# A state space's convolution input, taken out of the attention filler and given a phase of its own with seven products for four

## The chip, the cores and the metric

The kernel runs on one core of a Trainium2 chip. The metric is the device time of one execution in microseconds (us); lower is better. Before the change three runs took 2005.05, 2005.51 and 2002.23 us, median 2005.05.

The engines go by these names: PE is TensorE (matrix products; PEld its weight loads), DVE is VectorE, ACT is ScalarE, POOL is GpSimd, and SP is the queue that starts most DMAs.

## What is computed

One block of a hybrid encoder on x of 1024 tokens by 1024 features. The normalized input is multiplied by one wide matrix `w_in`; its columns feed latent attention (MLA, 8 heads), forgetting attention (fox, 8 heads), a Mamba-2 state space (SSD) and the gates that merge the three. Then an output projection and a gated FFN with a convolution. What the change touches is the input of the state space, 1536 columns, and the three gates, 3072 columns:

```python
hn = rms_norm(x, norm_mix_g[l])
u = hn @ w_in[l]
u_mla, u_fox, u_ssm, u_gate = jnp.split(u, split_at, axis=-1)
...
z, xBC, dt_raw = jnp.split(u, [SSM_INNER, SSM_INNER + SSM_XBC], axis=-1)
xBC = jax.nn.silu(causal_dwconv(xBC, conv_w, conv_b))
...
g = jax.nn.sigmoid(u_gate + b_gate[l]).reshape(Bsz, S, N_BRANCH, D_MODEL)
```

`causal_dwconv` has four taps along the tokens, a weight of its own for each column and tap.

## The kernel before, in words

Every float32 product is made of three passes on PE: both operands are split into a rounded high part (h, made by ACT) and the rest (l, made by DVE), and h·h, h·l and l·h are summed in PSUM. The normalized input, transposed, stays in SBUF as `hnh` and `hnl`, each in two halves of 512 tokens and 8 slices of 128 features. One block of 128 output columns costs 2 halves x 8 slices x 3 passes = 48 matmuls of 128x128 by 512.

The stages in time: norm and MLA projections to about 200 us; four chunks of 512 columns for fox and z, eight token units each (L798), to 384; attention to about 903; the state space to 1094; the branch outputs (L1729), the output projection (L1865), the FFN up (L1820) and down (L2161). In the chunks, `gate_sums` makes the forget gates' running sums on DVE, `down_sums` makes sums of FFN down weights on POOL at the units that `DOWN_FOX` lists, `out_z` finishes a z unit with a tanh, and `qk_sum`, `qk_pair` and `qk_out` normalize, transpose and split the fox queries and keys. In the FFN up projection, pairs of column blocks are made by seven half-size block products in place of eight (Strassen-Winograd), from sums of weights and of tokens.

**Attention** walks 16 heads, each in four units of two rows of 128 queries. A row of scores (`score_row`, matmuls L1296) has one chunk up to row four and two chunks from row five on, in a ring of three PSUM banks, tag "s". DVE takes the maximum of a chunk (L1301 for the first, L1312 for the last), the smaller of two negated ones (L1314), ACT the exponential (L1319), which frees the bank, DVE the sum's reciprocal (L1324, L1325), POOL the normalization (L1326). Later PE transposes (L1384), ACT and DVE split (L1389, L1390), and PE multiplies by the values (L1349 to L1357).

**The filler.** Between these matmuls stand others that depend on nothing in attention: `all_fill` makes 36 blocks, 12 of convolution input and 24 of gates, 48 matmuls each (L1179), as a generator. `merge` interleaves the streams of a unit by their share of work done; the filler's share is a number times the cost of the unit's own work, `FILL_ATT` in attention and `FILL_SSD` in the state space. The PE order is therefore written by the program; the orders of DVE, ACT, POOL and SP are chosen by a scheduler. A filled block is finished off PE: a gate by a tanh on ACT (L1158) and a store, a convolution block by `conv_done`: a copy (L1184), the bias and the first tap on POOL (L1144), three taps in two halves each on DVE (L1137), a tanh on ACT (L1150), a product on DVE (L1141). The weights of every block are split at L1122 (ACT) and L1123 (DVE).

Of the kernel before, what the change touches and what calls it, by code (L numbers as in the profile page):

```python
# [16 lines left out]
ALU = mybir.AluOpType  # L17
# [25 lines left out]
def block_kernel(ctx: ExitStack, tc: tile.TileContext, x, positions, norm_mix_g, w_in, b_gate,  # L43
# [83 lines left out]
    def uid(s):  # L127
        cnt[0] += 1
        return f"{s}_{cnt[0]}"
# [801 lines left out]
    def down_sums(tiles):  # L931
# [11 lines left out]
        for c, s_ in ((0, s12), (2, s34)):  # L943
            down_stores.append(lambda c=c, s_=s_: tc.keep_in_program_order(
                SY.dma_start(wsum_d[k, :, c:c + 2, :], s_)))

    with ExitStack() as px:
        xp = px.enter_context(TP("xp", 2))
# [21 lines left out]
        def getter(w, n, i):  # L970
            if n % 2:
                return lambda k: w[i][:, k, :]
            return lambda k: w[0][i][:, k, :] if k < 4 else w[k // 2 - 1][i][:, k % 2, :]

        def out_z(p, t, zc):
            th = xp.tile([P, 512], F32, name=uid("th"), tag="fsq")
            A.activation(th, p, AF.Tanh, scale=0.5)
            zt = xp.tile([P, 512], F32, name=uid("zt"), tag="fqn", bufs=4)
            V.scalar_tensor_tensor(out=zt, in0=th, scalar=1.0, in1=p, op0=ALU.add, op1=ALU.mult)
            SY.dma_start(z_d[t * P:(t + 1) * P, zc:zc + 512], zt)  # L980

        def qk_sum(p, ss):
            sq = xp.tile([P, 512], F32, name=uid("fsq"), tag="fsq")
            A.activation(sq, p, AF.Square)
            V.reduce_sum(ss, sq.rearrange("p (h d) -> p h d", d=64), axis=AX)
# [31 lines left out]
        for n, (which, c0) in enumerate(chunks):  # L1017
            wh, wl = getter(w, n, 0), getter(w, n, 1)
            w = []
            for t in range(NT):  # L1020
# [24 lines left out]
                if units >= 8:  # L1045
                    next(sums, None)
    pf.close()
    pjp.close()
    order0.__exit__(None, None, None)


# [17 lines left out]


    psg = ctx.enter_context(ExitStack())
    psf = psg.enter_context(TP("psfill", 2, space=PSUM))
# [3 lines left out]
    def later(us, fn):  # L1076
        h = [clk[0] + us, uid(""), fn]
        queue.append(h)
        return h
# [45 lines left out]

    def conv_done(j, u, ul, t0):
        a, al = f_t4.get()
        t = [t0]

        def step(us, fn):  # L1130
            h = later(t[0], fn)
            t[0] += us
            return h

        def tap(d, c0, c1):
            w = pc_g[:, 24 + 12 * (3 - d) + j:25 + 12 * (3 - d) + j]
            return lambda: pin(V.scalar_tensor_tensor(out=a[:, c0:c1], in0=u[:, c0 - d:c1 - d], scalar=w,  # L1137
                                                      in1=a[:, c0:c1], op0=ALU.mult, op1=ALU.add))

        def out(c0, c1):  # L1140
            return lambda: pin(V.scalar_tensor_tensor(out=u[:, c0:c1], in0=u[:, c0:c1], scalar=1.0, in1=a[:, c0:c1],  # L1141
                                                      op0=ALU.add, op1=ALU.mult))

        step(1.4, lambda: G.tensor_scalar(a, u, pc_g[:, 60 + j:61 + j], pc_g[:, 72 + j:73 + j],  # L1144
                                          op0=ALU.mult, op1=ALU.add))
        for d in (1, 2, 3):
            for c0, c1 in ((512, S), (d, 512)):
                step(2.0, tap(d, c0, c1))
        for c0, c1 in ((0, 512), (512, S)):
            step(1.6, lambda c0=c0, c1=c1: pin(A.activation(u[:, c0:c1], a[:, c0:c1], AF.Tanh)))  # L1150
        step(1.1, out(0, 512))
        al[0] = step(1.0, out(512, S))
        ul[0] = step(0.0, lambda: SY.dma_start(xbc_d[j], u))

    gate_behind = [None]
# [6 lines left out]
    def all_fill():  # L1162

        conv = [("c", j, C_XBC + j * P) for j in range(12)]
        gates = [(b, j, C_G + b * D + j * P) for b in (1, 0, 2) for j in range(NK)]
        blocks = [e for n in range(12) for e in (conv[n], gates[n])] + gates[12:]
        nxt = fill_load(blocks[0][2], True)
        for n, (kind, j, c0) in enumerate(blocks):
# [5 lines left out]
            for half in range(2):  # L1174
                ps, pl = f_ps.get()
                hs = slice(512 * half, 512 * half + 512)
                for k in range(NK):
# [3 lines left out]
                    if (k + 1) % grain[0] == 0 and k < NK - 1:  # L1181
                        yield 0.65 * grain[0]
                if kind == "c":
                    fn = lambda ps=ps, hs=hs, u=u: A.activation(u[:, hs], ps, AF.Copy)  # L1184
                else:
                    fn = lambda ps=ps, hs=hs, u=u, r=8 * kind + j: gate_tanh(u[:, hs], ps, pc_g[:, r:r + 1])
                wait = 50.0 if n == len(blocks) - 1 and half == 1 else 0.0
                pl[0] = later(wait + 1.4, fn)
                if half == 1:
                    if kind == "c":  # L1190
                        conv_done(j, u, ul, 2.2)
                    else:
                        ul[0] = later(wait + 2.0, lambda u=u, g=g_d[kind][j]: SY.dma_start(g, u))
                yield 0.65 * grain[0]
# [226 lines left out]

    FILL_ATT = 1.08
    FILL_SSD = [11.3] * 8 + [12.0, 24.5]
# [790 lines left out]
```

## Time and profile before

| what | us |
|---|---|
| median of three runs | 2005.05 |
| span of the profiled execution (a run of 2005.05 has some 3 us around it) | 2002.0 |
| PE busy | 1977.5 |
| DVE, ACT, POOL busy | 1365.9, 944.5, 651.9 |
| filler matmuls L1179, share of the chain that ended last | 19% |
| chunks of fox and z | about 198 to 384.5 |
| attention | 384.5 to about 903 |
| state space | about 904 to 1094 |

How to read the profile: one execution is recorded. A row of the timeline has start, length, engine, line, operation, what is written <- what is read, and in brackets the idle time ahead of it and what ended that. A row of the windows has the stretch, then busy time and number of instructions of PE, PEld, DVE, ACT and POOL, then the granted PE clock, the DMA share and GB/s. A row of groups has line, engine, operation, number | busy time, mean ns of one | idle time ahead and its releasers. A piece of the chain has start, length and what ran. Matmuls are pipelined: one of 512 columns shows as 390 ns and the next starts 227 ns after it.

### The profile page before, as it was taken

The numbers are of one execution on the slowest core, as the hardware profiler recorded it, in microseconds if no ns is written. First come the engines' busy times: TensorE is split into PE (matmuls) and PEld (weight loads), VectorE is DVE, ScalarE is ACT, GpSimd is POOL, SyncE is SP. The second block draws the span as 40 slices with busy tenths as digits, with TensorE's granted clock in tenths as the row PEclk, the third lists the DMA queues.
The fourth block names the chain that finished last, engine by engine and source line by source line (L and its number), as shares of the span: only waits on it lengthen the run. The fifth ranks groups of instructions, "written<-read, shape, count | busy, mean of one in ns | idle before, by whom it ended". The sixth has DMA issues, their size and how long they took to land.

```text
span 2002.0 us, 28702 instructions
## 1 busy us (share of the span) xinstructions
PE 1977.5 (99%) x10185; PEld 1676.7 (84%) x10185; DVE 1365.9 (68%) x2345; ACT 944.5 (47%) x1778; POOL 651.9 (33%) x636
## 2 busy tenths in 40 slices
PE   8999999999999999999999999999999999999998
PEld 7989888888888888888888888888888888888887
DVE  7777567267666677656885476568997777666665
ACT  5555323255555556557775132225454444544432
POOL 5133322021212223213331252100764544423764
PEclk9999999999999999999999999999999999999999
DMA  5166857543535444427654786433332211249575
GB/s 178 52 195 210 277 179 224 165 125 105 139 114 145 122 120 133 125 78 238 183 192 139 259 284 202 144 119 107 104 95 90 78 55 53 78 159 337 188 262 185
DMA packets 278265, 312.18 MB, mean 156 GB/s; under 512 B 19197, under 2 KB 209289, under 8 KB 278122
## 3 DMA queue, kind: packets, MB, share of 16 engines
q1 hardware_dynamic: 278120, 310.35, 49.6%
q8 instruction: 80, 1.31, 0.3%
q14 instruction: 63, 0.52, 0.1%
q10 hardware_dynamic: 2, 0.00, 0.0%
HBM read 217.17 MB, written 93.13 MB: 155 GB/s over the span
## 4 chain that ended last, share of the span: by engine, by line
PE 86%; DVE 4%; issue 3%; DMA 3%; POOL 2%; ACT 2%; SPq 1%; ACTq 0%; DVEq 0%; POOLq 0%
PE mm L1179 19%; PE fx L798 9%; PE dn L2161 8%; PE ybr L1729 7%; PE ua L1820 6%; PE uc L1820 5%; PE ud L1820 4%; PE wo L1865 4%; PE s L1296 4%; PE tp L1384 3%; PE ub L1820 2%; PE fxv L188 2%; PE py L1574 1%; PE o L1357 1%; PE ckv L517 1%
## 5 line engine op out<-in xcount | busy, mean ns | idle before, releaser
L1326 POOL TENSOR_SCALAR pm<-pm,rs 128x128 f32<-128x128 f32 (+7 forms) x128 | 105.3, 826 | 413.9 <-DVE rs L1325 290.1
L1179 PE MATMUL mm<-hnh,wh 128*128 128x512 f32 x576 | 236.9, 411 | 0.0
L1179 PE MATMUL mm<-hnh,wl 128*128 128x512 f32 x576 | 226.0, 392 | 0.0
L1179 PE MATMUL mm<-hnl,wh 128*128 128x512 f32 x576 | 225.8, 392 | 0.0
L2161 PE MATMUL dn<-dr,dr 128*128 128x512 f32 x592 | 182.3, 389 | 0.0
L1319 ACT ACTIVATE pm<-s,nmx 128x128 f32<-128x128 f32 (+2 forms) x192 | 110.4, 581 | 64.9 <-DVE nmx L1314 61.4
L2161 PEld LDWEIGHTS dn<-dr,dr 128*128 128x128 f32 x592 | 111.1, 188 | 23.0
L1179 PEld LDWEIGHTS mm<-hnh,wl 128*128 128x128 f32 x576 | 108.1, 188 | 24.6
L1179 PEld LDWEIGHTS mm<-hnl,wh 128*128 128x128 f32 x576 | 108.9, 189 | 15.6
L1179 PEld LDWEIGHTS mm<-hnh,wh 128*128 128x128 f32 x576 | 108.8, 189 | 15.5
L1390 DVE TENSOR_TENSOR ptl<-tp,pth 128x512 fp32r<-128x512 f32 (+1 forms) x160 | 98.4, 633 | 32.8 <-ACT pth L1389 30.7
L1389 ACT ACTIVATE pth<-tp 128x512 fp32r<-128x512 f32 (+1 forms) x160 | 84.8, 555 | 72.6 <-PE tp L1384 72.5
L2161 PE MATMUL dn<-dr 128*128 128x512 f32 x296 | 115.3, 389 | 1.1 <-DVE dY L2178 1.1
L135 DVE TENSOR_TENSOR dr<-dr,dr 128x1024 fp32r<-128x1024 f32 x52 | 75.8, 1465 | 49.1 <-ACT dr L134 47.2
L1729 PE MATMUL ybr<-ah,wl 128*128 128x512 f32 x256 | 99.7, 390 | 1.1 <-DVE wl L135 1.1
L1729 PE MATMUL ybr<-al,wh 128*128 128x512 f32 x256 | 99.8, 390 | 0.0
L1729 PE MATMUL ybr<-ah,wh 128*128 128x512 f32 x256 | 99.7, 389 | 0.0
L134 ACT ACTIVATE dr<-dr 128x1024 fp32r<-128x1024 f32 x52 | 55.1, 1061 | 73.0 <-PE dn L2161 50.0
L1312 DVE TENSOR_REDUCE nmx<-s 128x1 f32<-128x384 f32 (+3 forms) x128 | 65.8, 518 | 32.7 <-PE s L1296 19.1
L134 ACT ACTIVATE wh<-wr 128x1024 fp32r<-128x1024 f32 (+1 forms) x40 | 35.1, 877 | 98.1 <-PE ybr L1729 45.9
L1384 PE MATMUL tp<-ident,pm 128*128 128x128 f32 x576 | 79.8, 273 | 0.6 <-POOL pm L1326 0.6
L135 DVE TENSOR_TENSOR wl<-S,wh 128x1024 fp32r<-128x1024 f32 x42 | 63.2, 1504 | 23.3 <-ACT wh L134 23.3
(531 smaller groups left out, 5782.7 us busy)
## 6 DMA issues: line engine op xcount, KB each, us to landing
dr<-act_d SPq DMA_DIRECT2D x99, 256.0 KB
wr<-in_w_in_dram SPq DMA_DIRECT2D x36, 512.0 KB
g_d<-t SPq DMA_DIRECT2D x24, 512.0 KB
gl<-g_d SPq DMA_DIRECT2D x24, 512.0 KB
wr<-in_ffn_w_up_dram SPq DMA_DIRECT2D x23, 512.0 KB
ws<-in_ffn_w_down_dram SPq DMA_DIRECT2D x22, 512.0 KB
wsum_d<-ws SPq DMA_DIRECT2D x22, 512.0 KB
act_d<-fa SPq DMA_DIRECT2D x22, 512.0 KB
```

Source lines behind the costliest of these rows:

```text
L134: i = A.activation(h, src, AF.Copy) if he is A else he.tensor_copy(h, src)
L135: return i, le.tensor_sub(l, src, f32(h))
L798: T.matmul(p, a(k), b(k), start=k == 0 and i == 0, stop=k == NK - 1 and i == 2)
L1179: T.matmul(ps, a[:, k, :], b[half][:, k, :], start=(k == 0 and i == 0), stop=(k == NK - 1 and i == 2))
L1319: pss[cj][1][0] = later(t0 + 0.9 + 0.1 * cj, lambda cj=cj, a_=a_, b_=b_: A.activation(p_[:, a_:b_], pss[cj][0][:, :b_ - a_], AF.Exp, bias= ...
L1326: G.tensor_scalar(p_[:, 0:n * P], p_[:, 0:n * P], rs[:, 3:4], 0.0, op0=ALU.mult, op1=ALU.add)
L1384: T.transpose(pt[:, off:off + P], pn[qi][0][:, k * P:k * P + P], ident)
L1389: later(cs + 0.05, lambda th=th, pt=pt, off=off: A.activation(th[:, :off], pt[:, :off], AF.Copy))
L1390: pl[0] = later(cs + 0.6, lambda th=th, tl=tl, pt=pt, off=off: V.tensor_sub(tl[:, :off], pt[:, :off], f32(th[:, :off])))
L1729: T.matmul(pss[half], w_[:, k, :], a_[k][:, hs], start=k == 0 and i == 0, stop=k == nk - 1 and i == 2)
L1820: T.matmul(ps, a, b, start=first and n == 0, stop=n == 11, skip_group_check=not first)
L2161: T.matmul(ps[m], a[:, ts_], b[:, 512:], start=first_ and j == 0 and q == 0, stop=j == NFH - 1 and q == 2, skip_group_check=not first_)
```

## The change

The 12 convolution blocks leave the filler. They are made in a phase between the last chunk and attention, in six pairs: blocks n and n + 6, by seven products of 12 matmuls each with half the depth and half the tokens (504 matmuls, L1186 of the changed kernel, in place of 576). The token sums T1 to T4 that this needs are made by `token_sums` during the third and fourth chunk (DVE, two operations on POOL, ACT splits), the weights and sums of the first pair by `conv_first` in the fourth; so the gate sums are drained before the third chunk, and `DOWN_FOX` moves to earlier units. The convolution's taps run on full rows of 1024 on DVE, with bias and first tap on ACT and Silu in place of tanh and product. The filler is left with 24 gate blocks; `FILL_ATT` goes from 1.08 to 0.50, `FILL_SSD` stays. 588 of the filler's matmuls stand in attention (1206 before) and 564 behind it (522 before).

```diff
+    def token_sums():
...
+        u = {k: stage() for k in (0, 2)}
+        for k in (0, 2):
+            G.tensor_sub(u[k], b(hnl, 1, k + 4), b(hnl, 1, k))
+        yield
+        for k in (0, 2):
+            V.tensor_add(u[k], u[k], b(hnh, 1, k + 4))
+            V.tensor_sub(u[k], u[k], b(hnh, 1, k))
+            yield
+            fine(T3_, k, u[k])
+            yield
+        for k in (0, 2):
+            V.tensor_add(u[k], u[k], b(hnh, 0, k))
+            V.tensor_add(u[k], u[k], b(hnl, 0, k))
+            T4f.append(stage())
+            fine(T2_, k, u[k])
+            yield
+            V.tensor_sub(T4f[-1], b(hnh, 0, k + 4), u[k])
+            V.tensor_add(T4f[-1], T4f[-1], b(hnl, 0, k + 4))
+            V.tensor_sub(u[k], b(hnh, 1, k + 4), u[k])
+            V.tensor_add(u[k], u[k], b(hnl, 1, k + 4))
+            fine(T1_, k, u[k])
+            yield
...
-        DOWN_FOX = (2, 6, 10, 14, 18, 21)
+        DOWN_FOX = (1, 4, 7, 10, 13, 16)
...
+                if n == 2 and t >= 2 or n == 3:
+                    next(token3, None)
+                if n == 3:
+                    next(first_c, None)
...
+        def conv(j, c):
+            a = fpl.tile([P, S], F32, name=uid("ca"), tag="t4", bufs=4)
+            A.activation(a, c, AF.Identity, bias=pc_g[:, 72 + j:73 + j], scale=pc_g[:, 60 + j:61 + j])
+            for d in (1, 2, 3):
+                w = pc_g[:, 24 + 12 * (3 - d) + j:25 + 12 * (3 - d) + j]
+                V.scalar_tensor_tensor(out=a[:, d:], in0=c[:, :S - d], scalar=w, in1=a[:, d:],
+                                       op0=ALU.mult, op1=ALU.add)
+            A.activation(a, a, AF.Silu, scale=2.0)
+            SY.dma_start(xbc_d[j], a)
...
+        for n in range(6):
...
+            a0, b0, c0_, d0 = (c_bank() for _ in range(4))
+            c_product(a0, hA, 0, B11)
+            e1 = cg[:, 512:]
+            A.activation(e1, a0, AF.Copy)
+            steps_ = [lambda: c_product(b0, hS12, 4, T2c), lambda: c_product(a0, hA, 4, B21, False),
+                      lambda: c_product(c0_, hS12, 0, T1c)]
+            for i in (1, 2, 0) if n == 0 else (0, 1, 2):
+                steps_[i]()
...
-        conv = [("c", j, C_XBC + j * P) for j in range(12)]
-        gates = [(b, j, C_G + b * D + j * P) for b in (1, 0, 2) for j in range(NK)]
-        blocks = [e for n in range(12) for e in (conv[n], gates[n])] + gates[12:]
+        blocks = [(b, j, C_G + b * D + j * P) for b in (1, 0, 2) for j in range(NK)]
...
-    FILL_ATT = 1.08
+    FILL_ATT = 0.50
```

Three places in the orders. The first is on PE, inside attention's fifth head: rows five and six of its scores. Before, with `s_6413` the second chunk of row five, `s_6420` and `s_6440` the two chunks of row six:

```order
L1296 MATMUL s_6413<-w0h_5800,w0l_5801 128x256 x3
L1296 MATMUL s_6420<-w0h_5800,w0l_5801 128x384 x3
L1349 MATMUL o<-pth_6354,vv_5696 128x256
L1351 MATMUL o<-pth_6354,vv_5696 128x256
L1352 MATMUL o<-ptl_6355,vv_5696 128x256
L1357 MATMUL o<-ptl_6355,vv_5696 128x256
L1179 MATMUL mm_6364<-hnh_119,wh_5982 128x512
L1179 MATMUL mm_6364<-hnl_121,wh_5982 128x512
L1179 MATMUL mm_6364<-hnh_119,wl_5983 128x512
...
L1296 MATMUL s_6440<-w0h_5800,w0l_5801 128x384 x3
```

The same place now, with `s_7091`, `s_7099` and `s_7111` in these roles:

```order
L1441 MATMUL s_7091<-w0h_6561,w0l_6562 128x256 x3
L1441 MATMUL s_7099<-w0h_6561,w0l_6562 128x384 x3
L1494 MATMUL o<-pth_7039,vv_6477 128x256
L1496 MATMUL o<-pth_7039,vv_6477 128x256
L1497 MATMUL o<-ptl_7040,vv_6477 128x256
L1502 MATMUL o<-ptl_7040,vv_6477 128x256
L1441 MATMUL s_7111<-w0h_6561,w0l_6562 128x384 x3
```

The six filler matmuls between the two chunks of row six are gone; the four value matmuls (o) are still there.

The second place is on DVE, in the fourth chunk, ahead of the last normalized keys (`fqn`; `fr` and `rs_t` belong to their root, `fsl` are the split keys of the pair before). Before:

```order
L166 TENSOR_TENSOR rs_t_4352<-fr_843_4338 128x16
L167 TENSOR_TENSOR rs_t_4352<-rs_t_4352,rs_v_4342 128x16
L168 SCALAR_TENSOR_TENSOR fr_843_4338<-rs_t_4352,fr_843_4338 128x16
L994 TENSOR_TENSOR fqn_4356<-fx_4239,fr_843_4338 128x512
L994 TENSOR_TENSOR fqn_4358<-fx_4295,fr_843_4338 128x512
```

Now, with the token sums `Tf` and the low part `T2l` among them:

```order
L140 TENSOR_TENSOR T2l<-Tf_4190,T2h 128x1024
L1074 SCALAR_TENSOR_TENSOR fsl_4459<-tp_4453,fk_col,fsh_4458 128x512
L972 TENSOR_TENSOR Tf_4611<-Tf_4611,hnl_120 128x1024
L168 SCALAR_TENSOR_TENSOR fr_845_4356<-rs_t_4366,fr_845_4356 128x16
L157 TENSOR_SCALAR rs_i_4472<-fv_865_4469 128x16
L160 TENSOR_SCALAR rs_v_4475<-fv_865_4469 128x16
L973 TENSOR_TENSOR Tf_4190<-hnh_119,Tf_4190 128x1024
L166 TENSOR_TENSOR rs_t_4370<-fr_845_4356 128x16
L158 TENSOR_SCALAR fr_866_4471<-rs_i_4472 128x16
L974 TENSOR_TENSOR Tf_4190<-Tf_4190,hnl_121 128x1024
...
L1062 TENSOR_TENSOR fqn_4374<-fx_4267,fr_845_4356 128x512
```

Operations of 1024 elements now stand between the small ones of the root that the keys need.

The third place is on DVE where attention begins. Before, after the last z units (`zt`):

```order
L979 SCALAR_TENSOR_TENSOR zt_4732<-th_4730,fx_4705 128x512
L979 SCALAR_TENSOR_TENSOR zt_4762<-th_4760,fx_4735 128x512
L1312 TENSOR_REDUCE nmx_4836<-s_4838 128x1
L1312 TENSOR_REDUCE nmx_4844<-s_4846 128x1
L1325 RECIPROCAL rs_4837<-rs_4837 128x1
```

Now, with `cg_5563` and `cv_5659` the last pair's two blocks and `ca` their convolutions:

```order
L1247 TENSOR_TENSOR cg_5563<-cb_5566,X_5645 128x512
L1197 SCALAR_TENSOR_TENSOR ca_5665<-cg_5563,pc_g,ca_5665 128x1023
L1248 TENSOR_TENSOR cv_5659<-cb_5567,X_5645 128x512
L1197 SCALAR_TENSOR_TENSOR ca_5665<-cg_5563,pc_g,ca_5665 128x1022
L1197 SCALAR_TENSOR_TENSOR ca_5665<-cg_5563,pc_g,ca_5665 128x1021
L1197 SCALAR_TENSOR_TENSOR ca_5672<-cv_5659,pc_g,ca_5672 128x1023
L1197 SCALAR_TENSOR_TENSOR ca_5672<-cv_5659,pc_g,ca_5672 128x1022
L1197 SCALAR_TENSOR_TENSOR ca_5672<-cv_5659,pc_g,ca_5672 128x1021
L1457 TENSOR_REDUCE nmx_5750<-s_5752 128x1
```

Eight operations of the last pair now stand between the product phase and the first maximum.

More of the change, by code (lines that the diff above doesn't have):

```diff
@@ L1124, in fill_load @@
         return h, l, rl
[L1126 to L1153, printed above, removed]
     gate_behind = [None]
@@ L1189, in all_fill @@
                 if half == 1:
[L1190 to L1193, printed above, removed]
+                    ul[0] = later(wait + 2.0, lambda u=u, g=g_d[kind][j]: SY.dma_start(g, u))
                 yield 0.65 * grain[0]
```

136 lines of the change are left out of this document (127 added, 9 removed).

## The prediction

> **What bounds the kernel now.** I read the page first: engine totals, then the chain of work that ended last.
>
> ```profile
> span 2002.0 us, 28702 instructions
> PE 1977.5 (99%) x10185; PEld 1676.7 (84%) x10185; DVE 1365.9 (68%) x2345; ACT 944.5 (47%) x1778; POOL 651.9 (33%) x636
> PE 86%; DVE 4%; issue 3%; DMA 3%; POOL 2%; ACT 2%; SPq 1%; ACTq 0%; DVEq 0%; POOLq 0%
> ```
>
> TensorE is busy for 99% of the span, and the chain runs over it for 86%. So a matmul taken away is time taken away, as long as what is left still covers the waits that those matmuls cover today. The windows over the first part of attention show the same, with the other engines at about two thirds and a half, and the clock column at 1.00:
>
> ```profile
> 390.00:513.00 123.00, 121.52 (x709) 106.19 (x708) 81.32 (x195) 69.38 (x174) 29.30 (x37) 1.00 0.48 129
> ```
>
> The chain gives the price of one matmul of 512 columns: pieces of the filler in attention, and a long unbroken stretch.
>
> ```profile
> 384.68 5.44 PE mm L1179 x24
> 571.99 2.76 PE mm L1179 x12
> 1150.66 119.52 PE ybr L1729 x526
> ```
>
> 119.52/526 = 0.227 us in a long stretch, 2.76/12 = 0.230 us for twelve between other work. I work against the profiled execution, span 2002.0; the median of the runs is 2005.05, so 3.05 lies around the span, and I add it at the end.
>
> **Term A, the count.** The filler loses 12 blocks of 48 matmuls, 576. At 0.230 that is 132.5 us. The new phase issues 6 pairs x 7 products x 12 = 504 at 0.227, 114.4. Difference −18.1; there are also some 50 fewer places in attention where PE turns from transposes to filler, and I allow 0.03–0.05 us for each. **A = −20** (bounds −16.4, which is 72 x 0.227, and −22). The 42 filler matmuls that merely move from attention to the state space are in neither count.
>
> **Term B, chunk 3.** The token sums put 22 VectorE operations of 128x1024 beside the last two projection chunks, 21 of them between about 306 us and the last normalized keys. What VectorE does there today:
>
> ```profile
> 316.00:340.00 24.00, 24.00 (x115) 19.80 (x114) 19.79 (x42) 8.87 (x13) 8.39 (x7) 1.00 0.71 220
> 340.00:350.00 10.00, 10.00 (x50) 8.34 (x49) 8.83 (x21) 2.10 (x4) 3.64 (x2) 1.00 1.03 280
> 350.00:360.00 10.00, 10.00 (x49) 8.27 (x48) 2.67 (x4) 3.04 (x5) 0.00 (x0) 1.00 0.93 290
> ```
>
> ```profile
> L140 DVE TENSOR_TENSOR w5l<-raw,w5h 128x1024 fp32r<-128x1024 f32 x4 | 4.9, 1215 | 0.0
> L985 DVE TENSOR_REDUCE fss<-fsq 128x8 f32<-128x512 f32 x7 | 4.8, 682 | 6.9 <-ACT fsq L984 6.9
> ```
>
> VectorE (third pair) is busy for 19.79 of 24 and 8.83 of 10 already. In the order of after, 86 rows stand from the first token sum to fqn_4376: 21 of 128x1024 at about 1.15–1.2 (25 us), 7 reduces at 0.6, 7 fsl and 6 fqn at 0.6–0.7, some 45 small ones at 0.1–0.2: about 44 us without a gap. They can start at about 306, when GpSimd's two subtractions are there (they stand behind a load of down weights; today the same load leads to the GpSimd group at 315.97). So the last normalized keys are there at about 350–351. Today they are ready at 332:
>
> ```profile
> 331.43 1.29 DVE L994 TENSOR_TENSOR fqn<-fx,fr 128x512 f32<-128x512 f32 x2
> ```
>
> In the PE order their transposes stand right behind unit 24 of the 32, which ends at 339.20 + 5.50 = 344.7 (the next unit's piece is the second row):
>
> ```profile
> 339.20 5.50 PE fx L798 x24
> 345.58 5.47 PE fx L798 x24
> ```
>
> PE would have to wait from 344.7 to about 350.7; the 12 us of slack that cover this today are spent. **B = +6.** The lower bound is 3: the small operations, 45 of them, are taken 0.07 us shorter each. For the upper bound, what VectorE loses beside GpSimd:
>
> ```profile
> 317.23 1.30 POOL L940 TENSOR_TENSOR ws<-ws,ws 128x512 f32<-128x512 f32 x1
> ```
>
> ```profile
> 317.34 1.22 DVE L157 TENSOR_SCALAR rs_i<-fv 128x16 int32<-128x16 int32 x1
> 328.50 0.17 DVE L157 TENSOR_SCALAR rs_i<-fv 128x16 int32<-128x16 int32 x1
> ```
>
> The same small operation takes 1.22 us while a GpSimd subtraction runs and 0.17 without. Two loads of down weights, with four subtractions each, fall into the stretch; if three of the eight meet a small operation, 3 us more: 9. The Trainium skill, SBUF — State Buffer, "Who interferes with whom", has a rule for this: VectorE and GpSimd share a pair of ports under an exclusive lock, and the loser waits for the other's whole instruction. By that rule, the trace agrees in these three rows.
>
> **Term C, start of the phase.** In pair 0 the second product goes into the bank of the first (a0, first with B11 and then with B21), and must wait until ScalarE has copied the first out. That copy stands behind the last tanh and four splits, three of 1024 elements and one of 512:
>
> ```profile
> 384.72 0.60 ACT L977 ACTIVATE th<-fx 128x512 f32<-128x512 f32 x1 [4.84 <-PE fx L798]
> ```
>
> ```profile
> L134 ACT ACTIVATE wh<-S 128x1024 fp32r<-128x1024 f32 x20 | 21.2, 1062 | 31.3 <-PE uc L1820 31.3
> ```
>
> From the phase's start the copy ends after 0.6 + 1.06 + 0.6 + 2 x 1.06 + 0.6 = 5.0 us, the first product after 12 x 0.227 = 2.7. **C = +2.4** (1, if one split runs before the last tanh, to 4.5, if the two of T4 also wait for their VectorE half). The next product, waiting behind it on PE, needs T2 and a split that are long done.
>
> **Inside the phase** I charge nothing. Its nearest relative is the up projection of the FFN, which makes the same seven products per pair, with other sums:
>
> ```profile
> 1520.00:1600.00 80.00, 80.00 (x355) 66.24 (x354) 61.36 (x52) 38.96 (x46) 39.73 (x26) 1.00 0.25 80
> ```
>
> ```profile
> L2038 DVE SCALAR_TENSOR_TENSOR fa<-cg,pc_f,fa 128x1022 f32<-128x1022 f32 x11 | 24.4, 2216 | 0.0
> L2038 DVE SCALAR_TENSOR_TENSOR fa<-cv,pc_f,fa 128x1023 f32<-128x1023 f32 x11 | 14.0, 1273 | 0.0
> L2046 ACT ACTIVATE fa<-fa 128x1024 f32<-128x1024 f32 x11 | 11.7, 1061 | 16.1 <-DVE fa L2038 16.1
> ```
>
> 84 x 0.227 = 19.07 us a pair for PE. In those 80 us (4.2 pairs) VectorE is busy 14.6 us a pair, GpSimd 9.5, ScalarE 9.3, and PE never pauses. The convolution adds two taps (1.27 to 2.22 us each) and drops one product of 1.28: 15.9 to 17.8 a pair, under 19.07.
>
> **Term D, start of attention.** The last pair's tail (two sums, six taps) stands on VectorE ahead of attention's first maximum; on ScalarE two Silu and a table load stand ahead of the first exponential.
>
> ```profile
> L2046 ACT ACT_TABLE_LOAD x1 | 1.3, 1283 | 0.0
> ```
>
> Two sums of 0.7 (the reduce of 512 above takes 0.68) and six taps of 1.27–1.4 make 9.3 to 9.8 us behind the last product, less one us that starts before its end; after the taps, the last Silu (1.06), the table (1.28) and the first exponential: 10.8 to 11.3 us. PE has 24 filler matmuls (5.45), three scores (1.2) and six filler matmuls (1.36), 8.0 us, until it needs a score bank back. **D = +4** (2 to 7, the upper end with three of the taps at 2.2). Today none of it stands there.
>
> **Term E, the score banks in attention.** This term decides. The scores have three banks. A row from the fifth on has two chunks, and the exponential of its first chunk needs the maximum of its second. So the second chunk of the sixth row, which takes the bank of the fifth row's first, comes only after: second chunk's matmuls, its maximum, the minimum, the exponential, PE. The stretch, in head 4:
>
> ```profile
> 525.20 1.04 PE L1296 MATMUL s<-w0h,w0l 104*128 104x256 f32 x6
> 525.76 0.42 DVE L1312 TENSOR_REDUCE nmx<-s 128x1 f32<-128x256 f32 x1 [0.60 <-PE s L1296]
> 526.22 0.16 DVE L1314 TENSOR_TENSOR nmx<-nmx 128x1 f32<-128x1 f32 x1
> 526.47 0.58 ACT L1319 ACTIVATE pm<-s,nmx 128x384 f32<-128x384 f32 x1 [1.91 <-DVE nmx L1314]
> 526.56 0.40 PE L1179 MATMUL mm<-hnh,wh 128*128 128x512 f32 x1
> 527.95 1.38 PE L1296 MATMUL s<-w0h,w0l 104*128 104x384 f32 x6
> ```
>
> The exponential ends at 527.05, PE comes at 527.95: 0.9 us to spare. Of what lies between, six filler matmuls take 526.56 to 527.95. In the order of after they are gone from this place. PE would come at 526.56, 0.49 before the exponential's end, and wait 0.7 us with the 0.2 that pass until the next matmul runs (from 535.58, the end of the exponential in the first row below, to 535.78). The place recurs once in each of 16 heads: 16 x 0.7 = 11. A second place is the last chunk of a head, which needs the bank of the seventh row's first chunk. There the trace has a wait even now, with six filler matmuls ahead of it:
>
> ```profile
> 534.89 0.69 ACT L1319 ACTIVATE pm<-s,nmx 128x512 f32<-128x512 f32 x1 [2.45 <-DVE nmx L1314]
> 535.72 0.53 PEld L1296 LDWEIGHTS s<-w0h,w0l 104*128 104x128 f32 x3 [0.21 <-ACT pm L1319]
> 535.78 0.91 PE L1296 MATMUL s<-w0h,w0l 104*128 104x512 f32 x3
> ```
>
> By the order the filler is missing there in 7 of 16 heads; six matmuls of 0.23 were 1.4 us of cover, of which some 0.3 is won back by maxima that come sooner: 1.1 x 7 = 7.5. Shorter ones in the forgetting heads, which make a chunk in two matmuls in place of three, add about 2. Against this stands the convolution work that leaves VectorE, some 54 + 16.5 + half of 29.5 = 85 us of its busy time in attention, and what PE waits for such banks today, 6.0 us:
>
> ```profile
> L1137 DVE SCALAR_TENSOR_TENSOR t<-t,pc_g,t 128x512 f32<-128x512 f32 (+1 forms) x72 | 54.0, 752 | 0.5 <-POOL t L1144 0.2
> L1123 DVE TENSOR_TENSOR wl<-wr,wh 128x1024 fp32r<-128x1024 f32 x24 | 29.5, 1228 | 1.1 <-ACT wh L1122 1.1
> L1141 DVE SCALAR_TENSOR_TENSOR t<-t,t 128x512 f32<-128x512 f32 x24 | 16.5, 710 | 0.0
> ```
>
> ```profile
> PEld s L1296 <- ACT pm L1319: 6.0, 14, 1.3
> ```
>
> 20.5 less some of these 6: **E = +18** (8 to 27: the lower end if only half the places wait, the upper if each place waits 0.3 us more, as queueing on ScalarE would make it). The transposes behind the normalization keep 0.6 us or more, the values 3 us; I charge nothing there.
>
> **Sum.** −20 + 6 + 2.4 + 4 + 18 = +10.4, span 2012.4, with 3.05 around it **2015.5 us**. With all bounds at one end: −22+3+1+2+8 = −8, or −16.4+9+4.5+7+27 = +31; so 1997 to 2036.
>
> **Rivals.**
> 1. *The filler that is left covers the scores* (faster). E falls to nothing if the exponential of a fifth row's first chunk ends 1.36 − 0.2 = 1.16 us after the second chunk's matmuls begin, when PE comes back (525.20 to 526.56); the measured figure is 1.85 (525.20 to 527.05). For it: VectorE loses 85 of about 340 us of work there (81.32 in the first 123 us). Against it: the links of the chain (0.42, 0.16, 0.58) are bare durations, with little queueing in them. Then −20 + 12.4 = −7.6, 1997.5 us; if B is covered also, 1991.5. Chance 0.22.
> 2. *Waits breed waits* (slower than forecast). A late score delays maxima and normalizations behind it on VectorE and GpSimd, and transposes come late too; E goes above 27 and B above 9: 2031 to 2045. For it: no filler is left between. Against: the rows show GpSimd idle for most of attention. 0.08.
> 3. *The phase is bound by VectorE and GpSimd together.* If their operations only take turns, 16.8 + 9.5 = 26.3 us a pair against PE's 19.07, 6 x 7.2 = +43, about 2058. Against it: in the FFN 14.6 + 9.5 = 24.1 exceeds 19.07, and PE has no gap. It decides only if busy times there contain no waiting; the 2.22 us of the tap at L2038 against 1.28 shows that they contain it. 0.03. This is what the exclusive lock in the Trainium skill, SBUF — State Buffer, "Who interferes with whom", would do if every pair of operations met; the FFN rows speak against it.
> 4. *The gain and the stalls cancel*: E at 8–12 with B covered gives 2001 to 2009. 0.12.
>
> That the change doesn't do what it says is excluded by the order: 72 matmuls fewer, the filler's places as said.
>
> **How the numbers follow.** Forecast, 2009 to 2031, 0.55; rivals 0.22, 0.08, 0.03, 0.12. A measurement of this kernel can tell about 0.2%, 4 us. Faster than 2001: 0.22 and 0.02 of the edges, 0.24. Slower than 2009: 0.55 + 0.08 + 0.03 − 0.02 = 0.64. The same: 0.12. The range takes in most of rival 1: 1991 to 2031; the forecast's own is 2009 to 2031.
>
> **What would show it.** A: the filler's 1152 matmuls and 504 of the new line at 0.227. B: a gap on PE at about 345 behind VectorE's normalized keys. C: one wait of 2 us on ScalarE's copy in the first pair. D: a wait of some 4 us for an exponential with the first head. E: waits of PE for score banks of 15 to 25 us in all over attention, mostly the sixth row's second chunk. The prediction is wrong if the waits at the score banks sum to under 8 us, or if PE waits within the phase.

## The result, and the profile after

The changed kernel took 2049.4 us (median of four runs, 2047.28 to 2053.88) against 2003.64 for the kernel before (2001.98 to 2005.51): ratio 1.0226, 95% interval 1.0207 to 1.0245. It is 2.3% slower. The forecast, 2015.5, had the sign and a quarter of the size.

The page of the changed kernel, totals and the chain that ended last:

```profile
span 2045.5 us, 28760 instructions
PE 1982.2 (97%) x10113; PEld 1671.7 (82%) x10113; DVE 1411.8 (69%) x2341; ACT 976.0 (48%) x1802; POOL 687.6 (34%) x662
PE 77%; DVE 10%; issue 4%; ACT 4%; DMA 3%; POOL 1%; SPq 1%; ACTq 0%; DVEq 0%; POOLq 0%
```

PE has 72 matmuls fewer and is busy 4.7 us longer, in a span that is 43.5 us longer. Its share of the chain falls from 86% to 77%: DVE and ACT now stand in it for 10% and 4%. Waits of PE, whole program, in us, times, longest:

```profile
PE s L1441 <- ACT pm L1464: 20.6, 24, 2.2
PE tp L1069 <- DVE fqn L1062: 8.2, 1, 8.2
...
PE tp L1529 <- DVE ptl L1535: 3.2, 8, 1.0
PE o L1494 <- DVE o L1512: 2.2, 4, 1.0
PE cb L1186 <- ACT e L1236: 2.2, 4, 0.6
PE cb L1186 <- ACT cg L1230: 1.8, 1, 1.8
```

These are the score banks (first row), the token sums (second), transposes and values (next two), and the new phase (last two). In attention before the change the same view has:

```profile
PE o L1349 <- DVE o L1367: 1.6, 1, 1.6
PE s L1296 <- ACT pm L1319: 0.8, 1, 0.8
PE tp L1384 <- POOL pm L1326: 0.6, 1, 0.6
```

Each stage goes here from its first matmul to the first of the next one, and attention to its last value matmul. So cut, the two profiled executions stand as follows (us):

| stage | before | after | difference |
|---|---|---|---|
| norm, MLA projections | 198.3 | 197.9 | −0.4 |
| four projection chunks | 186.2 | 196.5 | +10.3 |
| new phase, 504 matmuls | – | 119.8 | +119.8 |
| attention, 1206 and 588 filler matmuls | 517.7 | 416.5 | −101.2 |
| state space, 522 and 564 | 191.9 | 208.3 | +16.4 |
| all behind it | 907.9 | 906.5 | −1.4 |

I take 0.2305 us for a filler matmul, between the 0.230 of the prediction and 0.231, the median from one to the next in attention before the change. At that price attention should have become 618 x 0.2305 = 142.4 us shorter and the state space 42 x 0.23 = 9.7 longer. So attention loses 41.2 us more than before, and the state space 6.7; waits are most of it, and halved clocks the rest.

**The chunks.** The timeline of PE around the last transposes of the keys, and of DVE:

```profile
344.18 0.39 PE L798 MATMUL fx<-w5h,hnl 128*128 128x512 f32 x1
352.74 1.94 PE L1069 MATMUL tp<-ident,fqn 128*128 128x128 f32 x8 [8.17 <-DVE fqn L1062]
354.32 0.78 PE L798 MATMUL fx<-w5h,hnh 128*128 128x512 f32 x1
354.90 0.63 PE L798 MATMUL fx<-w5l,hnh 128*128 128x512 f32 x1
```

```profile
350.35 1.22 DVE L974 TENSOR_TENSOR Tf<-Tf,hnl 128x1024 f32<-128x1024 f32 x1
351.49 0.17 DVE L167 TENSOR_TENSOR rs_t<-rs_t,rs_v 128x16 f32<-128x16 f32 x1
351.57 0.17 DVE L166 TENSOR_TENSOR rs_t<-fr 128x16 f32<-128x16 f32 x1
351.69 0.18 DVE L168 SCALAR_TENSOR_TENSOR fr<-rs_t,fr 128x16 f32<-128x16 f32 x1
351.78 0.17 DVE L167 TENSOR_TENSOR rs_t<-rs_t,rs_v 128x16 f32<-128x16 f32 x1
351.90 1.29 DVE L1062 TENSOR_TENSOR fqn<-fx,fr 128x512 f32<-128x512 f32 x2
```

The keys come at 352 to 353 instead of the 350.7 that was forecast. What had not been forecast stands in the next rows: the matmul after the wait takes 0.63 us, not 0.39. The windows around it have the granted clock in the third column from the end:

```profile
344.00:348.00 4.00, 0.57 (x3) 0.14 (x1) 4.00 (x8) 0.60 (x1) 0.00 (x0) 1.00 0.31 78
348.00:352.00 4.00, 0.00 (x0) 0.00 (x0) 4.00 (x13) 0.00 (x0) 0.00 (x0) 0.69 0.26 66
352.00:356.00 4.00, 3.27 (x12) 3.01 (x13) 3.19 (x9) 1.98 (x3) 0.00 (x0) 0.50 0.03 9
356.00:360.00 4.00, 4.00 (x18) 3.24 (x18) 3.37 (x7) 0.34 (x1) 2.23 (x2) 0.95 0.72 183
```

PE waits from 344.4; some five us later its clock is halved, and stays so until about 356.4, some four us after work has resumed. That is 2 us on top of the 8.3. The Trainium skill, TensorE: Matmul & The Clock Gate, "What's actually happening", says that an idle window of about 3.4 us halves the clock and a busy one of that length restores it; by that rule, the trace agrees here, but waits of 2.0 us halved it too (last section), and there the measurement decides.

**Attention.** The place that the prediction showed, now with the four value matmuls alone between the row's chunks, and the end of the same head:

```profile
579.22 1.06 PE L1441 MATMUL s<-w0h,w0l 104*128 104x256 f32 x6
580.49 0.28 PE L1502 MATMUL o<-ptl,vv 128*128 128x256 f32 x1
580.49 0.58 ACT L1464 ACTIVATE pm<-s,nmx 128x384 f32<-128x384 f32 x1 [1.92 <-DVE nmx L1459]
581.22 1.50 PE L1441 MATMUL s<-w0h,w0l 104*128 104x384 f32 x6 [0.46 <-ACT pm L1464]
...
586.52 0.33 PE L1502 MATMUL o<-ptl,vv 128*128 128x256 f32 x1
...
587.36 0.69 ACT L1464 ACTIVATE pm<-s,nmx 128x512 f32<-128x512 f32 x1
588.19 1.00 PE L1441 MATMUL s<-w0h,w0l 104*128 104x512 f32 x2 [1.34 <-ACT pm L1464]
```

The last value matmul starts at 580.49 and takes its place for 0.11 us; the next score starts at 581.22, after the exponential that ends at 581.07. PE loses 0.62 us at the sixth row's second chunk (0.7 was forecast), and by the same reckoning 1.5 us at the head's last chunk, 586.52 to 588.19 (1.1 was forecast). A wait at the first place recurs in all 16 heads and one at the second in 7, as the prediction had it.

### The profile page after: what moved, and what is told of

Same layout as the page of the kernel before. It is cut to its first block, busy times and chain, and to the rows that moved or that the text cites. A ratio compares the mean times of both kernels' runs of the same rounds, so it can differ in the third digit from the quotient of the medians.

```text
span 2045.5 us, 28760 instructions
## 1 busy us (share of the span) xinstructions
PE 1982.2 (97%) x10113; PEld 1671.7 (82%) x10113; DVE 1411.8 (69%) x2341; ACT 976.0 (48%) x1802; POOL 687.6 (34%) x662
## 4 chain that ended last, share of the span: by engine, by line
PE 77%; DVE 10%; issue 4%; ACT 4%; DMA 3%; POOL 1%; SPq 1%; ACTq 0%; DVEq 0%; POOLq 0%
PE mm L1330 11%; PE dn L2306 10%; PE ybr L1874 7%; PE fx L798 6%; PE ua L1965 5%; PE uc L1965 5%; PE ud L1965 4%; PE wo L2010 4%; PE s L1441 4%; PE tp L1529 3%; PE cb L1186 2%; PE ub L1965 2%; PE fxv L188 2%; DVE ca L1197 1%; ACT pm L1464 1%
## 5 line engine op out<-in xcount | busy, mean ns | idle before, releaser
L1471 POOL TENSOR_SCALAR pm<-pm,rs 128x128 f32<-128x128 f32 (+7 forms) x128 | 95.8, 751 | 309.3 <-DVE rs L1470 156.4
L1330 PE MATMUL mm<-hnh,wh 128*128 128x512 f32 x384 | 161.4, 420 | 0.0
L1330 PE MATMUL mm<-hnl,wh 128*128 128x512 f32 x384 | 151.9, 396 | 0.0
L1330 PE MATMUL mm<-hnh,wl 128*128 128x512 f32 x384 | 151.9, 396 | 0.0
L135 DVE TENSOR_TENSOR wl<-S,wh 128x1024 fp32r<-128x1024 f32 x53 | 79.5, 1499 | 27.3 <-ACT wh L134 27.3
L134 ACT ACTIVATE wh<-S 128x1024 fp32r<-128x1024 f32 x53 | 56.1, 1059 | 70.7 <-PE uc L1965 47.1
L134 ACT ACTIVATE wh<-wr 128x1024 fp32r<-128x1024 f32 (+1 forms) x45 | 40.3, 896 | 102.4 <-PE ybr L1874 51.9
L1330 PEld LDWEIGHTS mm<-hnh,wl 128*128 128x128 f32 x384 | 73.1, 190 | 16.9
L1330 PEld LDWEIGHTS mm<-hnl,wh 128*128 128x128 f32 x384 | 73.5, 191 | 11.6
L1330 PEld LDWEIGHTS mm<-hnh,wh 128*128 128x128 f32 x384 | 73.4, 191 | 11.5
```

Of the source, the lines that this page charges most:

```text
L134: i = A.activation(h, src, AF.Copy) if he is A else he.tensor_copy(h, src)
L135: return i, le.tensor_sub(l, src, f32(h))
L1330: T.matmul(ps, a[:, k, :], b[half][:, k, :], start=(k == 0 and i == 0), stop=(k == NK - 1 and i == 2))
L1471: G.tensor_scalar(p_[:, 0:n * P], p_[:, 0:n * P], rs[:, 3:4], 0.0, op0=ALU.mult, op1=ALU.add)
```

## The experiments

All are compared with the kernel before, in the same batch. Stage times are cut as in the table above.

### Is it the thin filler, or the rest of the change?

Two kernels from the two sides. The first takes the kernel before and thins its filler only:

```diff
-    FILL_ATT = 1.08
+    FILL_ATT = 0.525
...
             run_until(clk[0] + 3.0)
+            for _ in range(103):
+                advance(fill)
+            owed[0] = 0.0
+            run_until(clk[0] + 12.0)
     pw0.close()
```

> The kernel before, with the filler in attention thinned as in the changed kernel (582 matmuls up to attention's last value product in place of 1206) and the 624 that are missing made in one stretch between attention and the state space; no phase of its own, no token sums. Theory 1 (the thin filler uncovers waits in attention, whatever else is changed): attention takes 374 us of matmuls plus 25 to 39 us of waits, the whole 2023 to 2040. Rival (the changed kernel's other work, on VectorE, ScalarE and the queues, makes the waits): under 8 us, the whole at most 2010.

Measured: 2057.74 us in one run, beside 2002.78, and over the 2040 of theory 1. Attention takes 415.6 us with 582 filler matmuls, where 517.7 − 624 x 0.2305 = 373.9 would be without new waits: 41.7 us of waits, as many as in the changed kernel, and some more than the 25 to 39 expected. (The stretch behind it takes 348.9 us where 191.9 + 624 x 0.227 = 333.5 was due, the rest of the excess; PE waits 4.3 us there for a load of the convolution's result.) The waits of PE are the same ones:

```profile
PE s L1296 <- ACT pm L1319: 19.1, 24, 1.9
PE stp L1510 <- issue: 5.6, 2, 3.3
PE tp L1384 <- DVE ptl L1390: 4.7, 9, 1.2
PE stp L1510 <- DMA t<-xbc_d: 4.3, 1, 4.3
```

The second takes the changed kernel and fills it up again:

```diff
-        blocks = [(b, j, C_G + b * D + j * P) for b in (1, 0, 2) for j in range(NK)]
+        gates = [(b, j, C_G + b * D + j * P) for b in (1, 0, 2) for j in range(NK)]
+        twice = [(b, j, c0) for b, j, c0 in gates[:12]]
+        blocks = [e for n in range(12) for e in (twice[n], gates[n])] + gates[12:]
...
-    FILL_ATT = 0.50
+    FILL_ATT = 1.08
```

> The changed kernel with the filler as dense as before: twelve gate blocks are computed a second time (into a scratch tensor that nothing reads) in the places of the twelve convolution blocks, and the share in attention is 1.08 again. That is 576 matmuls more, 133 us at 0.23. Theory 1 (waits in attention and in the state space are those that the filler covered): attention's waits fall from 48 to 9 to 15 us and the state space's from 26 to about 19, so the whole is 2047 + 133 - 40 = 2135 to 2142. Rival (the waits have other causes): 2170 to 2180.

Measured: 2131.1 us in one run, just under the 2135 to 2142 of theory 1. Attention takes 517.0 us and the state space 191.9, what they take in the kernel before, to 0.7 us. In the waits only one long one is left of the 24, that of the first head:

```profile
PE tp L1070 <- DVE fqn L1063: 8.2, 1, 8.2
PE stp L1654 <- issue: 2.5, 2, 1.4
PE s L1444 <- ACT pm L1467: 2.5, 1, 2.5
```

So thinning alone makes the loss in attention, and filling alone takes it away. The convolution work that left VectorE changes little: with the dense filler attention is 0.7 us shorter without it, the first head's wait of 2.5 us included. The two kernels with the same phase also give the price that the prediction should have used: 618 filler matmuls more cost attention 517.0 − 416.5 = 100.5 us, **0.163 us each on average, not 0.230**.

### Does it matter where the thin filler stands?

```diff
         for ci, (a, b) in enumerate(chunks):
+            if ci == 1 and i in (5, 7):
+                owed[0] -= advance(fill) or 0.0
             ps, pl = a_s.get()
```

> The changed kernel with the filler in attention put elsewhere, not more of it: one group of six filler matmuls stands right ahead of the second chunk of the sixth and of the eighth row of scores in each head, and the rest is thinned by as much. Theory 1 (the loss in attention is the wait for a score bank at these two places): these waits, some 0.7 us in 16 heads and 1.5 us in 8, nearly vanish, 15 to 20 us less than the changed kernel. Rival (PE has 40 us too little cover in attention wherever it stands): the waits reappear where the filler was taken, at transposes and values, and less than 6 us is gained.

Measured: 2052.36 us, ratio 1.0249 (1.0234 to 1.0265), against 1.0226 for the changed kernel: nothing gained. PE's waits for exponentials fall from 20.6 to 12.1 us, and the others take their place:

```profile
PE s L1443 <- ACT pm L1466: 12.1, 13, 2.5
PE tp L1531 <- DVE ptl L1537: 8.7, 15, 1.2
...
PE tp L1531 <- DVE rs L1472: 4.1, 5, 0.9
```

My theory that two places carry the loss fell here; the rival holds: with three score banks, cover was missing in sum.

### Banks, or the length of the chain?

The next ones stand on the kernel `tok_late` (below), 2036.21 us. A fourth score bank, at the price of one of the filler's two while attention runs:

```diff
-    psf = psg.enter_context(TP("psfill", 2, space=PSUM))
+    psf = psg.enter_context(TP("psfill", 1, space=PSUM))
...
-        a_s = Ring(psp, [P, 512], F32, "s", 3)
+        a_s = Ring(psp, [P, 512], F32, "s", 4)
```

> The kernel tok_late with a fourth PSUM bank for scores, taken from the filler, which has one bank in attention and two after it. Theory 1 (three banks are what PE waits for in thin attention): the waits for exponentials, some 25 us, fall under 6, attention takes 395 to 403 us instead of 418, the whole 15 to 20 us less than tok_late's 2036. Rival (the chain maximum, exponential, normalization, transposes has a length of its own, and any cover must come from other work): the waits move to transposes and values, or to the filler's one bank, and less than 6 us is gained.

Measured: 2019.49 us, ratio 1.0083 (1.0068 to 1.0098); attention 395.2 us for 418.2 in `tok_late`, with 12 filler matmuls fewer. The state space takes 4.9 us more. PE's longest waits in attention:

```profile
PE o L1495 <- DVE o L1513: 5.7, 9, 2.0
PE s L1442 <- ACT pm L1465: 4.3, 11, 1.8
```

The banks bind first. Some 20 of the 41 us go with one bank (23.0 less 2.8 for the 12 matmuls); what is left are shorter waits, the largest for the accumulator of the values, then exponentials (4.3) and transposes (2.9).

A longer lag, with transposes and values three units behind the scores and eight probability buffers:

```diff
-            for n in range(len(units) + 2):
+            for n in range(len(units) + 3):
...
-                if n >= 2:
-                    share += cost_v(done[n - 2][1])
+                if n >= 3:
+                    share += cost_v(done[n - 3][1])
```

> The kernel tok_late with the transposes and values of a unit three units behind its scores instead of two (eight probability buffers instead of six). Theory 1 (score banks bind, the lag doesn't): the waits for exponentials stay at some 25 us, those of transposes and values fall by some 5, the whole 2 to 6 us less than tok_late's 2036. Rival (the length of the chain over two units binds, and shows at the banks because they stand first): attention 12 to 25 us less.

Measured: 2043.36 us in one run, attention 425.5 us, 7 longer. Neither expectation was met. PE's waits for exponentials fall from 21.0 to 14.5 us, but those for the accumulator of the values grow from 3.1 to 18.6. Why, I did not follow up.

The kernel before with the fourth bank, the same edit in it:

> The kernel before, with its dense filler, and four score banks with one filler bank in attention. Theory 1 (the banks bind only where the filler is thin; here PE waits for an exponential 6 us in all): within 3 us of before. Rival (three banks cost something with any filler): 4 to 6 us faster. Should the one filler bank bind, it is slower by some 0.3 us in each of 50 half blocks, up to 15 us.

Measured: 2025.14 us, ratio 1.0109 (1.0094 to 1.0124), 1.1% slower and past the 15 us of the expectation. With dense filler it is the filler's one bank that binds; PEld waits 13.1 + 9.6 us for the copies and tanhs that empty it:

```profile
PEld mm L1179 <- ACT t L1184: 13.1, 8, 2.0
PEld mm L1179 <- ACT t L1158: 9.6, 8, 2.0
```

So banks are no gain by themselves: of the two splits tried, three and two are better with the dense filler, four and one with the thin one.

### The token sums

```diff
-                if n == 2 and t >= 2 or n == 3:
-                    next(token3, None)
+                if n == 3:
+                    for _ in range(1 if t == 0 else 2):
+                        next(token3, None)
```

> The changed kernel with one thing moved: all token sums are made during the fourth chunk (z units, VectorE nearly idle there) instead of from the third chunk's third unit on. Theory 1 (the token sums delay the normalized keys; PE waits 8.3 us and then runs at half clock for some 6 us): the wait of the key transposes goes, the granted clock stays 1.00 through the chunks, the chunks take 186 to 188 us instead of 196.6, the whole 9 to 11 us less than the changed kernel's 2047. Rival (VectorE has not the time for the sums anywhere before the phase, so they only end later and the phase starts late): the chunks or the first pair of the phase wait instead, less than 3 us gained.

Measured: 2036.21 us, ratio 1.0175 (1.0158 to 1.0192). The chunks take 186.4 us, 0.2 more than before the change; the phase still takes 119.9. PE has no wait where the keys are transposed, and its clock stays at 1.00 (a window of `tok_late`):

```profile
340.00:360.00 20.00, 20.00 (x97) 16.61 (x97) 14.31 (x22) 7.04 (x11) 0.00 (x0) 1.00 0.56 156
```

Nearly the whole 10.3 us was the place of the token sums, the half clock included.

### Sharing the filler

```diff
-    FILL_ATT = 0.50
-    FILL_SSD = [11.3] * 8 + [12.0, 24.5]
+    FILL_ATT = 0.75
+    FILL_SSD = [5.0] * 8 + [5.5, 11.0]
```

> The kernel tok_late with the same 1152 filler matmuls shared otherwise: 842 up to attention's last value product (588 before), 310 behind it. Theory 1 (a filler matmul costs its 0.23 us less what it covers, and the cover is worth about as much in attention as in the state space): attention 40 to 48 us longer for 254 matmuls more (58 us of them), the state space 35 to 45 shorter, the whole within 8 us of tok_late's 2036. Rival (attention is the only place that wants it): the state space 55 to 58 us shorter, the whole 12 us or more below.

Measured: 2080.99 us, ratio 1.039 (1.0375 to 1.0406); both expectations wrong. Attention is 49.6 us longer for 254 matmuls more, and the state space with 254 fewer only 3.1 shorter. The state space has no slack to give up: PE waits, and its clock falls. The windows over the state space of this kernel (with 12 us of attention ahead of it) and of `tok_late`:

```profile
960.00:1180.00 220.00, 177.10 (x929) 150.43 (x928) 143.49 (x194) 132.87 (x280) 67.57 (x80) 0.88 0.48 153
```

```profile
930.00:1120.00 190.00, 183.81 (x1017) 156.50 (x1016) 141.55 (x184) 131.70 (x276) 58.00 (x79) 1.00 0.57 177
```

The other way, 66 matmuls moved to the state space (`FILL_ATT` 0.44, `FILL_SSD` [12.2] * 8 + [13.0, 26.0]), three score banks:

> The kernel tok_late, with three score banks, and the share 0.44 in attention (522 matmuls, 66 moved to the state space). Theory 1 (with three banks attention is out of cover: what is taken there comes back as waits at the banks): attention less than 8 us shorter for 15 us of matmuls, the state space 5 to 12 us longer, the whole 0 to 6 us above tok_late's 2036. Rival (the state space is where cover is missing, whatever the banks): the whole 3 us or more below tok_late.

Measured: 2042.02 us, ratio 1.0183 (1.0166 to 1.02), within the error of `tok_late`'s 1.0175. Attention is 7.1 us shorter and the state space 13.7 longer, as theory 1 has it, though the state space goes past its 12: with three banks nothing is to be had from these two ways of sharing.

### The phase, and the best version found

Eight banks in the phase (`bufs=6` to `bufs=8` in `c_bank`):

> The kernel tok_late with eight PSUM banks in the new phase instead of six. Theory 1 (from the second to the fifth pair the first product of a pair waits 0.7 us for ScalarE's copy, because the bank comes back too late): these four waits go, the phase takes 117 us instead of 119.9, the whole 2 to 3 us less than tok_late. Rival (ScalarE is late with everything, the wait moves to the next product): no change within 1 us.

Measured: 2041.42 us, ratio 1.0187 (1.017 to 1.0204); the four waits are still there, 0.66 to 0.72 us each. My theory fell, and it had the place wrong: the four stand ahead of a pair's sixth product, not its first. That product adds into the bank of the fourth, which ScalarE must copy out first, so no further bank can help. That the copy comes late is seen in the changed kernel's ScalarE rows:

```profile
423.69 1.28 ACT L1199 ACT_TABLE_LOAD   x1 [3.98 <-DVE ca L1197]
424.98 1.06 ACT L1199 ACTIVATE ca<-ca 128x1024 f32<-128x1024 f32 x1
...
427.37 1.05 ACT L1199 ACTIVATE ca<-ca 128x1024 f32<-128x1024 f32 x1
428.32 1.04 ACT L134 ACTIVATE wh<-S 128x1024 fp32r<-128x1024 f32 x1
429.27 0.58 ACT L1236 ACTIVATE e<-cb 128x512 f32<-128x512 f32 x1
```

The pair before's Silu stands at the head of ScalarE's queue and waits 3.98 us for the taps; the copy that PE needs, L1236, comes behind it, at 429.27, for a product whose last matmul ended at 426.70; PE is free at 429.26 and goes on at 429.90. Nor did the wait move to the next product, as the rival had it. The 5 us above `tok_late` need not come from the banks: one of the four runs, with a mean granted clock of 0.997, took 2036.45 us, and the other three, with 0.993 and 0.994, 2041.41 to 2042.25.

Four banks, the T4 splits behind the first copy, and 36 filler matmuls ahead of the first scores:

```diff
-            A.activation(e1, a0, AF.Copy)
+            tc.keep_in_program_order(A.activation(e1, a0, AF.Copy))
+            if n == 0:
+                for i, k in enumerate((0, 2)):
+                    split_here(*(e[:, k:k + 2, :] for e in T4_), T4f[i])
...
-            merge([], 5.0)
+            merge([], 8.0)
```

> The kernel banks4 with two small covers: the splits of the token sums T4 stand behind the first pair's first copy on ScalarE, and 36 filler matmuls instead of 24 stand ahead of attention's first scores. Theory 1 (the first pair waits 2.0 us for a copy queued behind those splits; attention's first scores wait 2.0 and 1.1 us for exponentials queued behind the last pair's tail): both waits go but for some tenths, the whole 3 to 5 us less than banks4's 2019.5. Rival (the same chains end a little later and the waits move on): under 1.5 us.

Measured: 2020.53 us, ratio 1.0088 (1.0071 to 1.0105): no gain over `banks4`, as the rival has it. The first pair's wait falls from 2.0 to 0.85 us and the second pair's grows from 0.7 to 1.2; the phase goes from 119.9 to 119.1. The rest is not gained: attention takes 396.8 us after 395.2, the state space 213.7 after 210.1.

The same with 0.44, and with 0.34 (`FILL_SSD` [14.5] * 8 + [15.0, 27.0]):

> The kernel start with some 50 filler matmuls moved from attention to the state space (share 0.44). Theory 1 (with four score banks attention needs less cover, and the state space, which lost 45 us when 254 matmuls were taken from it, gains from more): attention 8 to 12 us shorter, the state space 6 to 12 longer, the whole 0 to 4 us below the kernel start. Rival (attention has no slack either, each matmul taken there comes back as a wait): the whole 3 us or more above.

> The kernel start_044 with some 116 more filler matmuls moved from attention to the state space (share 0.34). Theory 1 (with four score banks attention still has slack to give: from 0.50 to 0.44 it got shorter by 11.6 us for 52 matmuls, their full price, and the state space did not get longer): attention 20 to 26 us shorter, the state space 15 to 22 longer, the whole 4 to 10 us below start_044's 2014, that is 2004 to 2010. Rival (attention's slack ends here): attention less than 15 us shorter, the whole above 2014.

Measured: 2014.06 us, ratio 1.0057 (1.0042 to 1.0072), and 2018.3, ratio 1.0074 (1.0059 to 1.0089). At 0.44 attention is 11.6 us shorter for 52 matmuls, nearly their full price, and the state space with the branch outputs 4.0 us longer (212.1 + 180.6 after 213.7 + 175.1; the last 24 filler matmuls now stand behind the first branch product). That is better than theory 1 had it. At 0.34 attention is 15.7 us shorter again for 116 matmuls, where theory 1 had 20 to 26, and the two stages behind it 22.5 longer (239.8 + 175.4): past the best. So `start_044` is the best of the versions with the phase, some 35 us below the changed kernel and still 0.6% above the kernel before. None of those tried beats it.

## Why the prediction was wrong

The direction, the places and most of the sizes held; the term of the sum that failed is E, 18 in the forecast and some 39 us by the runs.

- **A**, −20: the count is exact. At full prices it gives 114.4 − 142.4 + 9.7 = −18.3 us; what the fewer switches saved, two us in the sum, no run shows apart.
- **B**, +6: 10.3. The mechanism was right (`tok_late` takes all of it away but 0.2 us). The wait was 8.3, within the bounds of 3 to 9; two more came from the halved clock, which no term and no rival had. Every row that I had read showed the clock at 1.00, but none of them had a long wait in it, and I had just forecast one.
- **C**, +2.4: 2.0 at its place. "Inside the phase I charge nothing" was 2.8 us short: four waits of 0.7 for a copy in ScalarE's queue. Busy sums per pair were right (PE was the bound); the order within a queue is not in them. This was one of the prediction's own signs of being wrong ("or if PE waits within the phase").
- **D**, +4: 2.4, the first wait for an exponential in the first head, within the bounds of 2 to 7. That head's sixth row waits 1.65 us too, but this belongs to the thin filler: `thin_before`, without the phase, has the same 1.65, and `dense_after`, with it, has none.
- **E**, +18: attention lost 41.2 us, D's 2.4 among them, so some 39 for E. As gaps of PE I count the time from one matmul's start to the next less what such a matmul usually takes, where 0.2 us or more is left. The score banks were sized well: the gaps ahead of scores that an exponential released add up to 25 us, 2.4 of them D's and 1.3 there before, so 21 are new, against 20.5 forecast before the deduction. The step that failed is "The transposes behind the normalization keep 0.6 us or more, the values 3 us; I charge nothing there". PE's gaps there add up to some 15 us against 3 before, the half clock from 588.5 to 595.3 us costs some 2, and the rest is spread over many gaps of a tenth or two. The slack had been counted from the kernel before, with its cover in it, for each place alone; `target` shows that the cover of one place is taken from another. Whether the deduction for the work that leaves VectorE was right stays open: `dense_after` gains 0.7 us in attention with D's 2.5 in it, and `thin_before`, which keeps half of that work there (36 of 72 taps), has 23.6 us of gaps at the score banks against 22.5 without D's.
- **State space**, 0: +6.7. I had counted moved matmuls only. Half clocks at 1008.3 and 1076.6 us, 3.4 us each, cost some 2.7, so some 4 are left for waits. `dense_after`, with the filler as before, has none of it; what in the thinner filler makes each of these waits I did not settle.
- Of the rivals, the second (waits breed waits, 2031 to 2045, chance 0.08) came nearest, E above 27 and late transposes included; but 2049.4 lies above it too, and neither it nor any other had the halved clock or the loss in the state space. The third is refuted: the phase runs at 119.8 us for 114.4 of matmuls.

## What to carry to other kernels

A filler matmul on a busy engine is not worth its own time when it is taken out. What it saves is its time less the wait that it covers, and here that was 0.163 of 0.230 us on average, so 576 fewer in the filler (94 us) could not pay for 504 more elsewhere (114). The price hangs on the buffers: with four score banks 52 matmuls taken out saved 11.6 us, nearly their full time. Slack that is counted at single places, with the cover still in it, did not show this loss; whether a sum over the whole chain would have, no run here shows. So test the thinning alone first, as `thin_before` does: that needs a changed constant and a place for the work that is moved, and no new phase.

## What was not expected of the hardware

The clock falls after waits much shorter than 8 us, and not every time. In the first pair of the phase PE waits 2.0 us in nine of the kernels here. In five of them (`dense_after`, `lag3`, `att_075`, `share_044`, `banks8`) the clock is halved right behind that wait, for 3.4 us; in the other four (the changed kernel, `target`, `tok_late`, `banks4`) it is not. `tok_late`, `lag3`, `att_075` and `share_044` run the same instructions up to there, so the kernel does not decide it; what does, these runs do not show. The windows of `tok_late`, then of `banks8`:

```profile
386.00:390.00 4.00, 2.79 (x12) 2.30 (x13) 2.48 (x3) 1.15 (x2) 0.00 (x0) 1.00 1.03 290
```

```profile
387.00:391.00 4.00, 3.01 (x9) 2.35 (x10) 2.36 (x2) 0.93 (x2) 0.00 (x0) 0.72 1.06 293
391.00:395.00 4.00, 4.00 (x17) 3.24 (x16) 1.49 (x1) 1.55 (x2) 3.39 (x3) 0.85 0.30 90
```

In the window of `att_075` above, PE was busy for 177 of 220 us and had 0.88 of its clock on average; in that of `tok_late`, with 254 filler matmuls more behind attention, it was busy for 184 of 190 and had 1.00. So here the filler covered waits and also kept the clock up.
